# Sample attention in twenty steps of 512 keys in place of forty of 256, with a ring of fourteen key/value tiles

## The chip, the core and the metric

The kernel runs on one core of a Trainium2 chip. The metric is the device time of one execution in microseconds (us). The core has a matrix engine (PE, with its weight loads shown apart as PEld), a vector engine (DVE), a scalar engine (ACT), GpSimd (POOL), and SyncE (SP), which issues most direct DMA transfers. Indirect transfers (gathers) are issued by POOL. Each engine works through its own instructions in a fixed order and waits where an operand isn't there yet.

## The reference, cut to what matters

The kernel computes one inference step of a hybrid layer: a joint input projection, RWKV-7 heads, attention heads with three branches (compressed, selected, window), an output projection with layer norm, and a PEER expert mixer with layer norm. There are 256 prompt tokens and 8 sample sequences of 4 new tokens with 2048 past tokens each. All arithmetic here is fp32. The change touches the selected and the window branch of the sample's attention:

```python
s = jnp.einsum('bqkgd,bqknld->bqkgnl', q_c, k_g)             # selected blocks
kpos = top_idx[..., None] * SEL_BLOCK + jnp.arange(SEL_BLOCK)
m = (top_val >= 0)[..., None] & (kpos <= qpos[None, :, None, None, None])
p_s = masked_softmax(s.reshape(B, qc, NSA_KV_HEADS, NSA_GROUP, top_n * SEL_BLOCK), ...)
o_sel = jnp.einsum('bqkgnl,bqknld->bqkgd', p_s..., v_g)
...
s = jnp.einsum('bqkgd,bjkd->bqkgj', q_c, wkv[:, :, 0])         # window of 512
p_w = masked_softmax(s, m[None, :, None, None, :])
o_win = jnp.einsum('bqkgj,bjkd->bqkgd', p_w.astype(dt), wkv[:, :, 1])
return g_c[..., 0:1] * o_cmp + g_c[..., 1:2] * o_sel + g_c[..., 2:3] * o_win
```

The kernel scores all 2048 past keys of a sequence, and adds to each score a bias that is very negative for blocks that were not selected, so the selected branch is 2048 past keys (and 4 new ones) with a mask; the window branch is 512 past keys and the new ones.

## The kernel before, in words

**Stages.** The program is a row of stages. In each, several streams of work (Python generators) are interleaved by `weave` according to weights: that gives the program's order, which is a priority. A list scheduler with a model of each engine's time then sets the order on each engine, keeping dependences, the number of buffers of each pool, and the PSUM banks. So a change of a step can move instructions of another stream.

**The stage of the change** (marked W3, lines 1562 to 1580) weaves two streams: the sample's attention (`sample_late`: first steps, compressed branch, then `sample_attention`) with weight 137, and the RWKV states and steps of the sample (`sample_states`, `sample_steps`, lines 1205 to 1310) with weight 54. In the profiled execution it runs from about 561 to about 763 us. The next stage (W4) attends the prompt's tokens and begins the output projection.

**Tiles of the attention.** Sequences are taken in four pairs (`bp`), and a pair has 8 steps of 256 selected keys and 2 steps of 256 window keys: 40 steps. A tile `co` is 128 partitions by 1024: 256 positions of one sequence, two positions to a partition (e = 0, 1), with keys of 4 heads in columns 0 to 255 and values in 256 to 511 of each. A step has two such tiles, one for each sequence of the pair (b2). Selected tiles come by a gather on POOL (line 448), window tiles by a direct transfer on SP (line 894). They live in a ring of 10 tiles, 4 in one pool and 6 (`NCX`) in another; a step asks for the tiles of up to two steps ahead (`NAHEAD`) when its keys are turned.

**A step**, with its lines:

- `keys`: four transposes a sequence on PE (two head pairs kp, two positions e, line 918) into a PSUM bank `sa`, then one copy of 128x512 to `kt` (line 919): by DVE for the first sequence, by ACT for the second.
- `scored`: four matmuls (b2, kp), each 32 query rows in a column group of PE of its own, into one bank `sc` (line 937); in the last step of a branch four more against the new keys (line 940), into the same bank. DVE spreads the bias (line 931), adds it and takes the maximum (line 941, 945), negates it (line 947 or 949); ACT takes the exponential and its sum (line 951), into `S`.
- `applied`: PE turns the weights (two transposes, line 960) into bank `st`, ACT copies them to `pt` (line 962, 964), PE multiplies them with the values (eight matmuls, line 968) into bank `sao`, and ACT copies the result to `Oc` (line 970).
- At the end of a branch the parts are merged by their maxima on DVE (line 974 to 981, one call of line 981 for each step); at the end of a pair of sequences `heads` turns the result (line 990 to 997).

The order in the stream is keys(i+1), applied(i), scored(i+1). PSUM has banks ss=2 (for the states), sa=2, sc=1, st=1, sao=2. The states' and steps' lines on PE are 1217, 1232, 1259, 1288, 1297 and 1305, all into `ss`; POOL makes a masked product for line 1297 at line 1295.

**SP's row** in this stage: states in (`big`, line 1213, two batches), the prompt's x for the next stage (line 1627), window tiles, states out (line 1310), and the gate's weights `cw` for the next stage (lines 1413, 1414).

Of the kernel before, what the change touches and what calls it, by code (L numbers as in the profile page):

```python
# [14 lines left out]
AF = mybir.ActivationFunctionType  # L15
# [19 lines left out]
NAHEAD = 2  # L35
# [8 lines left out]
NCX = 6  # L44
# [23 lines left out]
def _const_table():  # L68
# [50 lines left out]
    for kk in range(4):  # L119
        wm[:, 0, kk % 2, kk // 2] = np.where(kk >= i + 1, 0.0, NEG)  # L120
# [26 lines left out]
def hybrid_decode_step(ctx: ExitStack, tc: tile.TileContext, a, outs, dbg=None):  # L147
# [299 lines left out]
    def gather(dst, rows_, ix):  # L447
        gp.indirect_dma_start(out=dst, out_offset=None, in_=rows_, in_offset=bass.IndirectOffsetOnAxis(ap=ix, axis=0))  # L448
# [431 lines left out]
    units = [(br, bp, ck) for bp in range(4) for br in "sw" for ck in range(2 if br == "w" else 8)]  # L880
# [3 lines left out]
    def load(i):  # L884

        br, bp, ck = units[i]
        tiles[i] = []
        for b2 in range(2):
            pool, n_ = rings[nload[0] % len(rings)]
            nload[0] += 1  # L890
            t_ = pool([P, 1024], "co", bufs=n_)
            if br == "w":
                src = a["state_win_kv"][0, 2 * bp + b2, 256 * ck:256 * ck + 256]
                sy.dma_start(t_, src.rearrange("(p e) a h d -> p (e a h d)", e=2))
            else:
                gather(t_, rows_s, sidx[:, 2 * bp + b2, ck:ck + 1])
            tiles[i].append(t_.rearrange("p (e c) -> p e c", e=2))

    def sample_attention(sp):


        kts, prob, outp = {}, {}, {}

        def kind(i):
            br, bp, ck = units[i]
            return br, bp, ck, (1, 2) if br == "w" else (0, 8)

        def keys(i):
            for i_ in range(i, min(i + 1 + NAHEAD, 40)):
                if i_ not in tiles:  # L910
                    load(i_)
            kts[i] = [sp([P, 2, 256], "kt", bufs=4) for b2 in range(2)]
            for b2 in range(2):
                pb = bank("sa")
                for kp in range(2):
                    for e in range(2):
                        o = 256 * kp + 128 * e
                        pe.transpose(pb[:, o:o + 128], tiles[i][b2][:, e, 128 * kp:128 * kp + 128], ident)  # L918
                (sc.copy if b2 else ve.tensor_copy)(kts[i][b2].rearrange("p k n -> p (k n)"), pb)

        def scored(i):
            br, bp, ck, (br_, nck) = kind(i)
            kt, new = kts.pop(i), ck == nck - 1
            if not ck:
                outp[br] = sp([P, 3, nck], "ST" + br), sp([P, nck, P], "Oc" + br)
            ST = outp[br][0]
            if br == "w":
                mk = C4("wmask")[:, 256 * ck:256 * ck + 256].rearrange("p (e k) -> p e k", e=2)
            else:
                BX = sp([P, 4, 32], "BX", bufs=2)  # L930
                ve.tensor_copy(BX, BI[:, bp, 4 * ck:4 * ck + 4, None].to_broadcast([P, 4, 32]))
                mk = BX.rearrange("p a b -> p (a b)")[:, None, :].to_broadcast([P, 2, P])
            mx2 = sp([P, 2], "mx2", bufs=3)
            S = prob[i] = sp([P, 288], "S", bufs=3)
            pb = bank("sc")
            for cg, (b2, kp) in enumerate(CG):
                pe.matmul(pb[32 * cg:32 * cg + 32, :256], q_of(2 * bp + b2, kp), kt[b2][:, kp, :], start=True, stop=True)
            if new:
                for cg, (b2, kp) in enumerate(CG):
                    pe.matmul(pb[32 * cg:32 * cg + 32, 256:288], q_of(2 * bp + b2, kp), KN[:, br_, kp, :], start=True, stop=True)  # L940
            ve.tensor_tensor_reduce(out=S[:, :256].rearrange("p (e k) -> p e k", e=2),
                                    in0=pb[:, :256].rearrange("p (e k) -> p e k", e=2),
                                    in1=mk, scale=1.0, scalar=NEG, op0=OP.add, op1=OP.max, accum_out=mx2[:, 0:1])
            if new:
                ve.tensor_tensor_reduce(out=S[:, 256:], in0=pb[:, 256:288], in1=C4("nmask")[:, 32 * bp:32 * bp + 32],
                                        scale=1.0, scalar=NEG, op0=OP.add, op1=OP.max, accum_out=mx2[:, 1:2])
                ve.tensor_scalar(ST[:, 0, ck:ck + 1], mx2[:, 0:1], mx2[:, 1:2], -1.0, op0=OP.max, op1=OP.mult)
            else:
                ve.tensor_scalar(ST[:, 0, ck:ck + 1], mx2[:, 0:1], -1.0, None, op0=OP.mult)
            n = 288 if new else 256  # L950
            sc.activation(S[:, :n], S[:, :n], AF.Exp, bias=ST[:, 0, ck:ck + 1], accum_out=ST[:, 1, ck:ck + 1])

        def applied(i):
            br, bp, ck, (br_, nck) = kind(i)
            S, tl, (ST, Oc), new = prob.pop(i), tiles[i], outp[br], ck == nck - 1
            tiles[i] = None
            po, pb = bank("sao"), bank("st")
            ks_ = [(0, P), (1, P)] + ([(2, 32)] if new else [])
            for k, w in ks_:
                pe.transpose(pb[:w, 128 * k:128 * k + 128], S[:, 128 * k:128 * k + w], ident)  # L960
            pt = sp([P, 384], "pt", bufs=2)
            sc.copy(pt[:, :256], pb[:, :256])
            if new:
                sc.copy(pt[:32, 256:], pb[:32, 256:384])
            for k, w in ks_:
                for cg, (b2, kp) in enumerate(CG):
                    rhs = tl[b2][:, k, 256 + 128 * kp:384 + 128 * kp] if k < 2 else VN[br_][:, 128 * kp:128 * kp + 128]
                    pe.matmul(po[32 * cg:32 * cg + 32, :P], pt[:w, 128 * k + 32 * cg:128 * k + 32 * cg + 32], rhs,
                              start=(k == 0), stop=(k == ks_[-1][0]))
            sc.copy(Oc[:, ck, :], po[:, :P])  # L970
            if new:
# [8 lines left out]
                for k in range(nck):  # L980
                    ve.scalar_tensor_tensor(Oa[:, bp, :], Oc[:, k, :], ST[:, 2, k:k + 1], Oa[:, bp, :],
                                            op0=OP.mult, op1=OP.add)
# [16 lines left out]
        for i in range(-1, 40):  # L999
# [6 lines left out]
            if i < 39:  # L1006
                scored(i + 1)
                yield 1
            if i % 10 == 2 and i < 30:
                yield from sample_compressed(sp, i // 10 + 1)  # L1010
            if i % 10 == 0 and i:
                heads(i // 10 - 1)
        heads(3)
# [551 lines left out]
    more_banks(sa=2, sc=1, st=1, sao=2)  # L1565
# [12 lines left out]
    weave((late, 137), (seq(sample_states(sx), sample_steps(sx)), 54))  # L1578
# [520 lines left out]
```

## Time and profile before

| | |
|---|---|
| median of 3 runs | 2595.13 us (2588.27 to 2599.22) |
| profiled execution | 2602.22 us, span 2600.4 us, mean PE clock 0.93 |
| PE busy | 2328.9 us, 90% of the span |
| PEld busy | 1961.5 us, 75% |
| DVE busy | 1955.5 us, 75% |
| ACT busy | 1027.7 us, 40% |
| POOL busy | 1281.1 us, 49% |
| the stage of the change, 561 to 763 us | PE 178.59, DVE 123.50, ACT 90.49, POOL 70.06 us busy of 202 |

The windows view tells by stretches how long each engine was busy; the groups view puts together instructions of one line, operation and shape; the timeline lists what follows what on each engine. A fp32 matmul appears as two records on PE, a transpose as one. A group's duration includes its drain, which can lie over the next group's start: what a group really holds of PE is read from start to start.

### The profile page before, as it was taken

The page shows a single profiled execution, that of the slowest core. Times are in us where ns is not written, and L with a number is a line of the kernel's source. Part 1 is how long each engine was busy: PE and PEld are TensorE (multiplying, and loading weights), DVE is VectorE, ACT ScalarE, POOL GpSimd, SP SyncE. Part 2 cuts the span into 40 slices and gives each one's busy share as a digit, 9 for nine tenths or more (in the row PEclk, how much of TensorE's full clock was granted, in tenths as well). Part 3 has the DMA queues.
Part 4 walks back from the last instruction along what each step waited for, and adds up shares of the span by engine and source line. Part 5 has one row for each costly group of instructions (what it writes and reads, how often), then busy time and mean ns, then how long its engine had stood idle before and what let it go on. Part 6 is the DMA issues. An engine that isn't in the chain of part 4 may idle for free.

```text
span 2600.4 us, 47649 instructions
## 1 busy us (share of the span) xinstructions
PE 2328.9 (90%) x17612; PEld 1961.5 (75%) x17612; DVE 1955.5 (75%) x4360; ACT 1027.7 (40%) x1932; POOL 1281.1 (49%) x1327
## 2 busy tenths in 40 slices
PE   7989999979989997469799999996699799989996
PEld 7877898865555655358699999995677688878885
DVE  4789756554742538949988888889976689878988
ACT  3433222224432332210244444443566544434443
POOL 5677423232510107635544444445555577767772
PEclk9989999988986997779899999997899999999998
DMA  7877964467656867886499999997778699899994
GB/s 222 241 218 241 275 199 139 130 200 223 213 178 234 275 243 245 312 267 172 153 371 349 352 352 346 352 338 225 232 241 294 233 324 326 319 336 322 325 322 174
DMA packets 346650, 683.49 MB, mean 263 GB/s; under 512 B 81338, under 2 KB 204785, under 8 KB 345361
## 3 DMA queue, kind: packets, MB, share of 16 engines
q1 hardware_dynamic: 251505, 344.67, 40.9%
q0 software_dynamic: 94912, 335.77, 36.9%
q8 instruction: 139, 2.28, 0.3%
q14 instruction: 94, 0.77, 0.1%
HBM read 664.77 MB, written 23.88 MB: 265 GB/s over the span
## 4 chain that ended last, share of the span: by engine, by line
PE 66%; DVE 17%; DMA 8%; issue 4%; POOL 3%; ACT 2%; SPq 0%; DVEq 0%; POOLq 0%; ACTq 0%
PE pb L2024 19%; PE ph L1832 14%; PE pj L417 6%; PE pt L1826 4%; DMA co<-in_cache_cmp_kv,gidx 2%; PE pj L1790 2%; PE pa L1650 2%; DVE rows L1756 2%; DVE CA L471 2%; PE ss L1478 2%; PE sa L918 1%; PE pa L1906 1%; PE p L1061 1%; PE px L1876 1%; PE fs L1924 1%
## 5 line engine op out<-in xcount | busy, mean ns | idle before, releaser
L448 POOL DMA_INDIRECT rq<-in_peer_v,gi x256 | 374.7, 1463 | 170.4 <-issue 80.7
L448 POOL DMA_INDIRECT rows<-in_peer_u,gi x256 | 298.6, 1166 | 313.3 <-DVE rows L1756 282.8
L1832 PE MATMUL ph<-XHd,ul 128*128 128x256 f32 x1024 | 304.6, 297 | 18.1 <-DVE ul L1622 18.1
L1756 DVE SCALAR_TENSOR_TENSOR rows<-rows,x1a 128x1024 f32<-128x1024 f32 x256 | 309.3, 1231 | 5.7 <-DMA rows<-in_peer_u,gi 5.5
L1832 PE MATMUL ph<-XHd,uh 128*128 128x256 f32 x1024 | 297.4, 290 | 0.3 <-ACT uh L1621 0.3
L1832 PE MATMUL ph<-XLd,uh 128*128 128x256 f32 x1024 | 290.7, 284 | 0.0
L1621 ACT CAST uh<-pt 128x512 fp32r<-128x512 f32 x256 | 149.8, 587 | 277.6 <-PE ph L1832 203.6
L417 PE MATMUL pj<-XH,wh 128*128 128x288 f32 (+1 forms) x752 | 230.4, 307 | 12.3 <-DVE ss L747 7.0
L417 PE MATMUL pj<-XH,wl 128*128 128x288 f32 (+1 forms) x752 | 232.2, 309 | 9.3 <-DVE wl L412 6.5
L1622 DVE TENSOR_TENSOR ul<-pt,uh 128x512 fp32r<-128x512 f32 x256 | 176.0, 689 | 80.8 <-ACT uh L1621 72.9
L417 PE MATMUL pj<-XL,wh 128*128 128x288 f32 (+1 forms) x752 | 226.7, 302 | 0.0
L2024 PE MATMUL pb<-vl,ah 128*128 128x512 f32 x768 | 217.7, 392 | 0.3 <-DVE vl L2018 0.3
L2024 PE MATMUL pb<-vh,al 128*128 128x512 f32 x768 | 216.4, 390 | 0.0
L2024 PE MATMUL pb<-vh,ah 128*128 128x512 f32 x768 | 199.1, 395 | 16.3 <-ACT vh L2017 16.3
L1832 PEld LDWEIGHTS ph<-XHd,ul 128*128 128x128 f32 x1024 | 196.7, 192 | 20.2 <-DVE ul L1622 20.0
L410 ACT CAST wh<-wraw 128x512 fp32r<-128x512 f32 (+1 forms) x188 | 114.8, 616 | 234.7 <-PE pj L417 180.2
L1832 PEld LDWEIGHTS ph<-XHd,uh 128*128 128x128 f32 x1024 | 197.3, 193 | 0.8 <-ACT uh L1621 0.5
L1832 PEld LDWEIGHTS ph<-XLd,uh 128*128 128x128 f32 x1024 | 197.0, 192 | 0.0
L1998 DVE SCALAR_TENSOR_TENSOR fP<-rq,ge,fP 128x512 f32<-128x512 f32 x254 | 189.9, 748 | 2.4
L2024 PEld LDWEIGHTS pb<-vh,ah 128*128 128x128 f32 x768 | 146.3, 191 | 47.7 <-ACT vh L2017 17.3
L471 DVE SCALAR_TENSOR_TENSOR CA<-co,wbc,CA 128x256 f32<-128x256 f32 x248 | 131.8, 570 | 55.8 <-DMA co<-in_cache_cmp_kv,gidx 55.6
L2024 PEld LDWEIGHTS pb<-vl,ah 128*128 128x128 f32 x768 | 145.8, 190 | 31.3 <-DVE vl L2018 0.7
(852 smaller groups left out, 5546.6 us busy)
## 6 DMA issues: line engine op xcount, KB each, us to landing
ur<-in_peer_u SPq DMA_DIRECT2D x128, 512.0 KB
wraw<-in_w_in SPq DMA_DIRECT2D x152, 256.0 KB
cw<-in_w_out SPq DMA_DIRECT2D x32, 512.0 KB
wraw<-in_w_out SPq DMA_DIRECT2D x32, 512.0 KB
cw<-in_peer_wq SPq DMA_DIRECT2D x32, 512.0 KB
wraw<-in_peer_wq SPq DMA_DIRECT2D x32, 512.0 KB
wraw<-in_w_in SPq DMA_DIRECT2D x64, 128.0 KB
co<-in_state_win_kv SPq DMA_DIRECT2D x16, 512.0 KB
```

Source lines behind the costliest of these rows:

```text
L410: sc.copy(wh[:, :, :n], w[:, :, :n])
L417: last[2] = pe.matmul(pb[:n, :nt], wi[:, k, :n], xi[(o + k) // 8][:, (o + k) % 8, :nt], start=(o + k == 0 and wi is wh and xi is xh), stop ...
L448: gp.indirect_dma_start(out=dst, out_offset=None, in_=rows_, in_offset=bass.IndirectOffsetOnAxis(ap=ix, axis=0))
L471: ve.scalar_tensor_tensor(d_, x_, w_, d_, op0=OP.mult, op1=OP.add)
L1478: pe.matmul(pb[32 * q:32 * q + 32, :256], lhs(k), w[:, 256 * q:256 * q + 256], start=(k % 4 == 0), stop=(k % 4 == 3))
L1621: sc.copy(xh, pb)
L1622: return ve.tensor_tensor(xl, pb, xh.bitcast(F32), OP.subtract)
L1756: i_ = ve.scalar_tensor_tensor(r_, r_, 1.0, X1a[t], op0=OP.mult, op1=OP.mult, accum_out=h_)
L1826: pe.transpose(pb[:, 128 * e:128 * e + 128], w[:, 512 * q + 128 * e:512 * q + 128 * e + 128], ident)
L1832: mm = pe.matmul(ph[:, :NPR], wi[:, e, :], xi[:, 4 * q + e, :NPR], start=(q == 0 and e == 0 and wi is wh and xi is XHd), stop=(q == 1 and ...
L1998: ve.scalar_tensor_tensor(fP[t], r_, w_, fP[t], op0=OP.mult, op1=OP.add)
L2024: pe.matmul(acc[3 * t + q], wi[:, P * t:P * t + P], xi[:, 512 * q:512 * q + 512], start=(k == 0 and wi is ah and xi is vh), stop=(k == P - ...
```

## The change

The steps become 512 keys: per pair of sequences four of the selected branch and one of the window, 20 in all, each with four tiles (i, b2, c), c being the half.

- `keys`: for each sequence and each head pair one bank `sa` with four transposes (e, c), and one copy of 128x512: DVE for the first head pair, ACT for the second.
- `scored`: the four matmuls are 32x512 and fill the bank `sc`; the new keys' four go to a bank `st`. One maximum over 512, one exponential over 512 (or 544), `S` has two buffers in place of three.
- `turned`: the turn of the weights is now a part of its own: four transposes, one copy of 128x512; the new keys' piece goes through a bank `sa`.
- `applied`: sixteen matmuls (or twenty) and one eviction; merges have half as many calls.
- The order in the stream is keys(i+1), turned(i−1), scored(i), applied(i−1), then the loads of four tiles. The ring has 14 tiles (`NCX` 10); fourteen are asked for at the start.
- The banks are ss=2, sa=3, sc=1, st=1, sao=1, and the weight of the stream is 78 in place of 137.

Line numbers of the changed kernel differ: before the function they are one lower, in the states and the later stages nine higher (1297 becomes 1306, 1213 becomes 1222, 1627 becomes 1636).

```diff
-NAHEAD = 2
...
-NCX = 6
+NCX = 10
...
-        wm[:, 0, kk % 2, kk // 2] = np.where(kk >= i + 1, 0.0, NEG)
+        wm[:, kk % 2, 0, kk // 2] = np.where(kk >= i + 1, 0.0, NEG)
...
-    units = [(br, bp, ck) for bp in range(4) for br in "sw" for ck in range(2 if br == "w" else 8)]
+    units = [(br, bp, u) for bp in range(4) for br in "sw" for u in range(1 if br == "w" else 4)]
+    pieces = [(i, b2, c) for i in range(len(units)) for c in range(2) for b2 in range(2)]
...
+    def loads(upto):
+
+        for i, b2, c in pieces[nload[0]:upto]:
...
-            kts[i] = [sp([P, 2, 256], "kt", bufs=4) for b2 in range(2)]
+            kts[i] = [sp([P, 2, 512], "kt", bufs=4) for b2 in range(2)]
             for b2 in range(2):
-                pb = bank("sa")
                 for kp in range(2):
-                    for e in range(2):
-                        o = 256 * kp + 128 * e
-                        pe.transpose(pb[:, o:o + 128], tiles[i][b2][:, e, 128 * kp:128 * kp + 128], ident)
-                (sc.copy if b2 else ve.tensor_copy)(kts[i][b2].rearrange("p k n -> p (k n)"), pb)
+                    pb = bank("sa")
+                    for n, (e, c) in enumerate(EC):
+                        pe.transpose(pb[:, 128 * n:128 * n + 128], tiles[i, b2, c][:, e, 128 * kp:128 * kp + 128], ident)
+                    (sc.copy if kp else ve.tensor_copy)(kts[i][b2][:, kp, :], pb)
...
-            S = prob[i] = sp([P, 288], "S", bufs=3)
+            S = prob[i] = sp([P, 544], "S", bufs=2)
             pb = bank("sc")
             for cg, (b2, kp) in enumerate(CG):
-                pe.matmul(pb[32 * cg:32 * cg + 32, :256], q_of(2 * bp + b2, kp), kt[b2][:, kp, :], start=True, stop=True)
+                pe.matmul(pb[32 * cg:32 * cg + 32, :], q_of(2 * bp + b2, kp), kt[b2][:, kp, :], start=True, stop=True)
             if new:
+                pn = bank("st")
...
+        def turned(i):
+            br, bp, u, (br_, nu) = kind(i)
+            S, pt = prob.pop(i), sp([P, 640], "pt", bufs=2)
+            pb = bank("st")
+            for k in range(4):
+                pe.transpose(pb[:, 128 * k:128 * k + 128], S[:, 128 * k:128 * k + 128], ident)
+            sc.copy(pt[:, :512], pb)
...
+        loads(len(rings))
+        for i in range(-1, 21):
+            if i < 19:
                 keys(i + 1)
                 yield 1
-            if i >= 0:
-                applied(i)
+            if i > 0:
+                turned(i - 1)
+            if 0 <= i < 20:
+                scored(i)
                 yield 1
-            if i < 39:
-                scored(i + 1)
+            if i > 0:
+                applied(i - 1)
+                loads(4 * i + len(rings))
                 yield 1
...
-    more_banks(sa=2, sc=1, st=1, sao=2)
+    more_banks(sa=3, sc=1, st=1, sao=1)
...
-    weave((late, 137), (seq(sample_states(sx), sample_steps(sx)), 54))
+    weave((late, 78), (seq(sample_states(sx), sample_steps(sx)), 54))
```

**Order on PE, in the last third of the stage.** A row is a run of instructions of one kind: line, operation, output and input names, shape, and how many. Before, around the state products of line 1297:

```order
L937 MATMUL sc<-kt,Qb 32x256 x2
L918 MATMUL sa<-CT_61,co 128x128 x4
L937 MATMUL sc<-kt,Qb 32x256 x2
L918 MATMUL sa<-CT_61,co 128x128 x8
L937 MATMUL sc<-kt,Qb 32x256 x4
L918 MATMUL sa<-CT_61,co 128x128 x4
L1297 MATMUL ss<-uvm,UB 64x512
```

and with the change, at the end of those products:

```order
L914 MATMUL sa<-CT_61,co 128x128 x7
L933 MATMUL sc<-kt,Qb 32x512
L914 MATMUL sa<-CT_61,co 128x128
L933 MATMUL sc<-kt,Qb 32x512
L914 MATMUL sa<-CT_61,co 128x128 x3
L1314 MATMUL ss<-CT_61,S0T 128x128 x3
L914 MATMUL sa<-CT_61,co 128x128 x4
L933 MATMUL sc<-kt,Qb 32x512
L914 MATMUL sa<-CT_61,co 128x128
L933 MATMUL sc<-kt,Qb 32x512
```

A step's four scores stood in one run or in two pairs; here each of the four stands by itself, between transposes of keys.

**Order on SP, over the whole stage.** Before (`x_00` to `x_11` are the prompt's x, `co` the window tiles):

```order
L1213 DMA big<-in_state_rwkv 64x4x64 x16
L1627 DMA x_00_10095<-in_x_prompt 128x1024
L1627 DMA x_01_10096<-in_x_prompt 128x1024
L1627 DMA x_10_10097<-in_x_prompt 128x1024
L1627 DMA x_11_10098<-in_x_prompt 128x1024
L1213 DMA big<-in_state_rwkv 64x4x64 x16
L894 DMA co<-in_state_win_kv 128x1024 x12
```

and with the change, its start and its end apart:

```order
L1222 DMA big<-in_state_rwkv 64x4x64 x32
L893 DMA co<-in_state_win_kv 128x1024 x12
```

```order
L1319 DMA out<-S_9538 64x4x64 x4
L1636 DMA x_00_9719<-in_x_prompt 128x1024
L1636 DMA x_01_9720<-in_x_prompt 128x1024
L1636 DMA x_10_9721<-in_x_prompt 128x1024
L1636 DMA x_11_9722<-in_x_prompt 128x1024
L1422 DMA cw<-in_rwkv_g 128x1024
L1423 DMA cw<-in_rwkv_g 32x1024
```

The four x transfers moved from between the two batches of states to behind the last states out, just ahead of the gate's weights.

More of the change, by code (lines that the diff above doesn't have):

```diff
@@ L879, in hybrid_decode_step @@
     tiles, ends = {}, {}
[L880 removed]
+    units = [(br, bp, u) for bp in range(4) for br in "sw" for u in range(1 if br == "w" else 4)]
+    pieces = [(i, b2, c) for i in range(len(units)) for c in range(2) for b2 in range(2)]
     rings, nload = [(na, NCO)] * NCO, [0]
[L884 to L888, printed above, removed]
+    def loads(upto):
+        for i, b2, c in pieces[nload[0]:upto]:
+            br, bp, u = units[i]
             pool, n_ = rings[nload[0] % len(rings)]
@@ L899, in sample_attention @@
+            tiles[i, b2, c] = t_.rearrange("p (e c) -> p e c", e=2)
     def sample_attention(sp):
-        kts, prob, outp = {}, {}, {}
+        kts, prob, outp, turned_ = {}, {}, {}, {}
+        EC = [(e, c) for e in range(2) for c in range(2)]
         def kind(i):
-            br, bp, ck = units[i]
-            return br, bp, ck, (1, 2) if br == "w" else (0, 8)
+            br, bp, u = units[i]
+            return br, bp, u, (1, 1) if br == "w" else (0, 4)
         def keys(i):
-            for i_ in range(i, min(i + 1 + NAHEAD, 40)):
-                if i_ not in tiles:
-                    load(i_)
-            kts[i] = [sp([P, 2, 256], "kt", bufs=4) for b2 in range(2)]
+            kts[i] = [sp([P, 2, 512], "kt", bufs=4) for b2 in range(2)]
@@ L953, in applied @@
-        def applied(i):
[L954 to L965, printed above, removed]
-                for cg, (b2, kp) in enumerate(CG):
-                    rhs = tl[b2][:, k, 256 + 128 * kp:384 + 128 * kp] if k < 2 else VN[br_][:, 128 * kp:128 * kp + 128]
+                ve.tensor_scalar(ST[:, 0, u:u + 1], mx2[:, 0:1], -1.0, None, op0=OP.mult)
@@ new lines, in scored @@
+            n = 544 if new else 512
+            sc.activation(S[:, :n], S[:, :n], AF.Exp, bias=ST[:, 0, u:u + 1], accum_out=ST[:, 1, u:u + 1])
+        def turned(i):
+            br, bp, u, (br_, nu) = kind(i)
+            S, pt = prob.pop(i), sp([P, 640], "pt", bufs=2)
[3 more added lines that the diff above has]
+            sc.copy(pt[:, :512], pb)
+            if u == nu - 1:
+                pn = bank("sa")
+                pe.transpose(pn[:32, :128], S[:, 512:], ident)
+                sc.copy(pt[:32, 512:], pn[:32, :128])
+            turned_[i] = pt
@@ new lines, in applied @@
+        def applied(i):
+            br, bp, u, (br_, nu) = kind(i)
+            pt, (ST, Oc), new = turned_.pop(i), outp[br], u == nu - 1
+            po = bank("sao")
+            for k in range(5 if new else 4):
+                for cg, (b2, kp) in enumerate(CG):
+                    if k < 4:
+                        e, c = EC[k]
+                        w, rhs = P, tiles[i, b2, c][:, e, 256 + 128 * kp:384 + 128 * kp]
+                    else:
+                        w, rhs = 32, VN[br_][:, 128 * kp:128 * kp + 128]
@@ L968, in applied @@
                     pe.matmul(po[32 * cg:32 * cg + 32, :P], pt[:w, 128 * k + 32 * cg:128 * k + 32 * cg + 32], rhs,
-                              start=(k == 0), stop=(k == ks_[-1][0]))
-            sc.copy(Oc[:, ck, :], po[:, :P])
+                              start=(k == 0), stop=(k == (4 if new else 3)))
+            sc.copy(Oc[:, u, :], po[:, :P])
             if new:
```

46 lines of the change are left out of this document (19 added, 27 removed).

## The prediction, made before the result was known

> **What bounds the kernel now.** The change lies in one stage, the sample's attention woven with the RWKV steps of the sample (about 561 to 763 us of the profiled execution), so I read that stage first, in the table of windows. Its columns are the stretch, its length, the busy us (and instruction count) of PE, PEld, DVE, ACT and POOL, then PE's granted clock, the DMA share and GB/s.
>
> ```profile
> core 0: us, PE busy (x) PEld busy (x) DVE busy (x) ACT busy (x) POOL busy (x), PEclk, DMA share, GB/s
> ...
> 581.00:591.00 10.00, 5.43 (x58) 3.51 (x57) 2.99 (x17) 3.32 (x13) 4.05 (x5) 0.74 1.01 265
> ...
> 631.00:641.00 10.00, 10.00 (x162) 6.74 (x162) 4.22 (x24) 4.67 (x18) 3.75 (x4) 1.00 0.58 187
> ...
> 721.00:731.00 10.00, 7.92 (x85) 4.89 (x89) 3.63 (x16) 4.77 (x14) 5.19 (x6) 1.00 1.02 346
> 731.00:741.00 10.00, 8.54 (x95) 4.58 (x89) 3.58 (x13) 5.56 (x16) 2.29 (x3) 1.00 1.02 357
> ...
> 751.00:763.00 12.00, 6.26 (x94) 3.94 (x83) 11.46 (x50) 4.17 (x14) 0.00 (x0) 0.87 0.41 98
> sum 202.00, PE 178.59 PEld 104.00 DVE 123.50 ACT 90.49 POOL 70.06; mean PE 8.93 PEld 5.20 DVE 6.18 ACT 4.52 POOL 3.50
> ```
>
> PE is busy 178.59 of 202 us; DVE (123.5) and ACT (90.5) are far from full. The 23.4 us in which PE stands still are gathered in a few places: where the DMA share is 1.0 (581 to 591, 721 to 741) and in the tail, where DVE alone works (11.46 of 12 us). Next the groups of instructions of that stage, to see what PE and its helpers do for the attention (after the bar: busy us, mean ns | idle just before, and what ended it):
>
> ```profile
> L918 PE MATMUL sa<-CT,co 128*128 128x128 f32 x320 | 54.6, 299 | 4.9 <-issue 2.9 <-DVE kt L919 1.6 <-DMA co<-in_cache_sel_kv,sidx 0.2
> L448 POOL DMA_INDIRECT co<-in_cache_sel_kv,sidx x56 | 53.5, 955 | 86.5 <-PE sao L968 70.1 <-issue 6.3 <-PE st L960 4.2
> L937 PE MATMUL sc<-kt,Qb 128*32 128x256 f32 x320 | 43.0, 404 | 2.1 <-DVE mx L941 0.7 <-issue 0.4 <-ACT kt L919 0.4
> L968 PE MATMUL sao<-co,pt 128*32 128x128 f32 x640 | 28.8, 285 | 2.8 <-ACT pt L962 2.7
> L960 PE MATMUL st<-CT,S 128*128 128x128 f32 (+1 forms) x88 | 17.8, 291 | 6.0 <-ACT S L951 4.5 <-DVE STs L949 1.5
> ...
> L951 ACT ACTIVATE S<-S,STs 128x256 f32<-128x256 f32 (+1 forms) x32 | 16.4, 512 | 14.0 <-DVE STs L949 11.2 <-issue 1.1 <-DVE s L538 0.9
> L962 ACT COPY pt<-st 128x256 f32<-128x256 f32 x40 | 15.0, 375 | 11.9 <-PE st L960 8.6 <-PE sc L937 1.5 <-ACT S L951 0.6
> L941 DVE CUSTOM_DVE_ANT_1 S<-sc,BX 128x256 f32<-128x256 f32 x32 | 13.4, 420 | 29.0 <-PE sc L937 16.4 <-PE sa L918 5.6 <-PE sc L940 3.9
> L981 DVE SCALAR_TENSOR_TENSOR Oa<-Ocs,STs,Oa 128x128 f32<-128x128 f32 x32 | 12.1, 379 | 1.8 <-ACT Ocs L970 1.2
> ```
>
> PE's waits for this chain are small: 6.0 us before the turn (L960), 2.8 before the apply (L968), 2.1 before the scores (L937). The stage is bound by how much PE does, with some idle for data. So the sum is made in PE time, and the last view is PE's timeline, whose starts show what a group really occupies (the second column includes the drain, which overlaps the next group):
>
> ```profile
> 704.14 1.09 PE L918 MATMUL sa<-CT,co 128*128 128x128 f32 x8
> ...
> 705.17 1.07 PE L1297 MATMUL ss<-uvm,UB 64*64 64x512 f32 x2
> ...
> 706.16 0.64 PE L968 MATMUL sao<-co,pt 128*32 128x128 f32 x16
> ...
> 709.86 0.64 PE L937 MATMUL sc<-kt,Qb 128*32 128x256 f32 x8
> ...
> 710.42 0.66 PE L918 MATMUL sa<-CT,co 128*128 128x128 f32 x4
> ```
>
> ```profile
> 727.19 0.63 PE L937 MATMUL sc<-kt,Qb 128*32 128x256 f32 x4 [0.22 <-DVE kt L919]
> ...
> 727.75 0.66 PE L918 MATMUL sa<-CT,co 128*128 128x128 f32 x4
> ...
> 728.34 0.64 PE L968 MATMUL sao<-co,pt 128*32 128x128 f32 x16
> ...
> 728.91 0.44 PE L960 MATMUL st<-CT,S 128*128 128x128 f32 x2
> ...
> 729.18 0.60 PE L1305 MATMUL ss<-CT,S0T 128*128 128x128 f32 x4
> ```
>
> An fp32 matmul leaves two records, a transpose one. Four scores side by side (x8) hold PE from 709.86 to 710.42, 0.56 us; two (x4) from 727.19 to 727.75, also 0.56. **A group of scores costs the same however many of the four column groups are in it**, and the transposes behind it start only when it is over.
>
> **The change part by part.** *Scores.* Before, one copy hands over both head pairs of a batch, so a step's four scores come out of the order in one group (16 steps) or in two pairs (24 steps): 16 + 48 = 64 groups, times 0.56 = 35.8 us. Now each copy hands over one head pair of one batch, with four transposes between, and a score is 512 wide. Counted in the order of the changed kernel, 7 steps fall into four singles, 6 into a pair and two singles, 3 into two pairs, 4 stay whole: 28 + 18 + 6 + 4 = 56 groups. A two-pass 512-wide matmul holds PE from 705.17 to 706.16, 0.99 us (L1297, the nearest row; a 256-wide score at 0.56 doubled would be 1.12). 56 × 0.99 = 55.4. Against 35.8 that is **+19.6 us**. Had all twenty stayed whole it would be 20 × 0.99 = 19.8, a gain of 16. This is the term that decides: half as many steps, but nearly as many groups, each twice as long.
>
> [...]
>
> *Keys.* 320 transposes as before. Eight hold PE 1.03 us (704.14 to 705.17), four 0.59 (727.75 to 728.34), so four more cost 0.44, and a group has some 0.15 of its own. The order has 87 groups in place of 74: 13 × 0.15 = **+2.0**. *Turn and apply.* Turning goes from 40 groups to 30 of the same transposes, −10 × 0.15 = **−1.5** (two hold PE 0.27, 728.91 to 729.18: below the fit, so it may be less). Applying goes from 41 groups to 33, at the same 0.15 **−1.2**; a bound on the other side is that eight groups' full 0.57 (728.34 to 728.91) minus their work were saved, some −3. *New keys* now go to a bank of their own and stand alone eight times: 8 × 0.15 = **+1.2** at most. Sum on PE: 19.6 + 2.0 − 1.5 − 1.2 + 0.6 (half of the new keys' bound) = +19.5; with the favourable ends of turn and apply, and a few neighbouring scores overlapping their drain, +15. I take **+17**: 178.6 becomes some 196 us.
>
> *DVE and ACT.* Maximum, exponential, eviction and merge run 20 times in place of 40. Per step the fixed part goes: a merge (L981) does half its 32 calls less, 6 us; the maximum, exponential and turned eviction double in width and save only their overhead. Altogether perhaps 17 us on each of DVE and ACT. All of it lies under PE (123.5 and 90.5 of 202 busy); only where PE waits for this chain does it show, 6.0 + 2.8 + 2.1 us at most by the groups above. The new place of the turn (behind the next keys, one step later) aims at the same 10.9 us. Against it stands a longer tail: the last step's turn, apply, merge and head transposes follow each other over 512 keys, in a stretch where DVE was already the bound (11.46 of 12). I book −6 for the waits and +4 for tail and start (first scores need four tiles of keys in place of two): **−2**.
>
> *Ring.* Fourteen tiles, requested four at a time after an apply. The gathers are the same 56 and the window loads the same 16, so bytes don't change, and the two stretches at DMA share 1.02 stay as they are.
>
> ```profile
> 732.31 0.94 POOL L448 DMA_INDIRECT co<-in_cache_sel_kv,sidx  x1 [0.88 <-PE sao L968]
> ...
> 733.55 0.93 POOL L448 DMA_INDIRECT co<-in_cache_sel_kv,sidx  x1 [0.30 <-PE st L960]
> ```
>
> POOL issues a gather each 1.24 us (732.31 to 733.55), so four take 5 us, and PE has some 10 us a step (202/20). What is queued behind them on POOL is the masked product for the state steps (L1295), which waits up to 5 us for a burst; PE's state matmuls (L1297) have the attention to cover that. I book **0**, and price the other case below.
>
> *Queue of SP.* The prompt's x loads, 2 MB (L1627), move from the stage's start to its end:
>
> ```profile
> 565.82 4.94 SPq L1627 DMA_DIRECT2D x<-in_x_prompt  x4
> ...
> 757.14 0.48 SPq L1413 DMA_DIRECT2D cw<-in_rwkv_g  x1
> 761.59 0.34 SPq L1414 DMA_DIRECT2D cw<-in_rwkv_g  x1
> ```
>
> At the start they shared the DMA engines with the first tiles, which is a gain of a few us there; now they hold SP 4.94 us ahead of the weights of the next stage's gate (cw), which bounds the loss at 5. I book **0**, ±3.
>
> Total: 17 − 2 = **+15 us** on the profiled execution's 2602.2 us (its span is 2600.4), that is 2617. That execution was 7 us above the median 2595.1 of the runs shown, so I state **2610** on the median's basis.
>
> **The rivals.** *Faster: a lone score runs beside its neighbours.* If a score on one column group overlapped the transposes or state matmuls around it, what counts would be passes of the widest column group: 20 × 0.99 = 19.8 against 35.8, −16, and with −2 for waits and −2 for turn and apply some −20: **2575**. It decides when a score group's mean start-to-start time falls under 0.49: 56 × 0.49 = 27.4, 8.4 under the 35.8 of before, and the other terms (−2.6 on PE, −2 in waits) make it 13. For it: column groups do overlap among themselves. Against: behind a pair the transposes started only after the whole 0.56.
>
> *No difference: the added PE time falls into idle.* PE stands still 23.4 us. If DVE's and ACT's lighter load and the later turn close all the 10.9 us of waits and half of the DMA-bound idle, 17 − 11 − 5 leaves about 0 to +3: **2597**. For it: the list order put other work into most gaps already. Against: the idle lies at DMA share 1.0 and in the tail, where neither helps.
>
> *Much slower: the ring stalls.* Fourteen tiles hold three and a half steps; half of a step's tiles are asked for only after an apply that now comes a step later.
>
> ```profile
> POOL co L448 <- PE sao L968: 70.1, 14, 16.7
> ...
> 994.91 6.23 DMA cw<-in_peer_u,gi
> ```
>
> POOL waited 70.1 us for applies already (harmlessly), and a gather of another stage took 6.23 us to land when it stood on the path. If the last two tiles of each of some 16 steps come 2 us late, that is +30 on top: **2640**. Against: in the order, an apply and the first use of the tile it frees are mostly seven or more us of PE work apart, by the group prices above.
>
> **How the numbers follow.** Likeliest (PE pays for single scores): 0.47, 2610, own range 2600 to 2628. Overlap: 0.19, 2575. Absorbed: 0.22, 2597. Ring: 0.12, 2640. About 0.5%, 13 us, is what a measurement here tells from no change; 2582 to 2608 is "within". Slower is the ring and three quarters of the likeliest, 0.12 + 0.35 = 0.47; faster the overlap, with a little of it left inside, 0.18; the rest, 0.35, is within. The range reaches from 2584 (most of the absorbed case, not the overlap) to 2635 (not the full ring case).
>
> **What would show it.** Right: in the stage's windows PE busy near 195 with DVE near 106 and ACT near 73; the scores' line in the timeline mostly as x2 groups of 128x512, each about 1 us from the next start; the stage some 15 us longer; everything behind it shifted by that. Wrong: a single score's next instruction starting 0.3 us later (overlap); PE idle under 10 us with PE busy near 195 (absorbed); long "DMA co" releasers before key transposes (ring); a change in the stages behind 763 us larger than that in this one.

## The result, and the profile after

The changed kernel took 2628.4 us (median of 4 runs, 2622.4 to 2634.0), the kernel before on the same chip 2595.4 us. The ratio is 1.0127 (95% interval 1.0102 to 1.0152): slower by 33 us, where +15 was forecast. The two profiled executions differ by less, 2625.8 against 2600.4 us of span, 25.4 us. The table shows where these lie, by the first rows of PE's lines in both traces:

| piece | before, us | after, us | difference |
|---|---|---|---|
| up to the stage | 559.9 | 558.8 | −1.1 |
| the stage of the change (to the first instruction of the next stage) | 202.1 | 214.1 | +12.0 |
| from there to the sample's first gate product (L1454, after L1463) | 2.8 | 11.7 | +8.9 |
| from the gate product to the end of the sample's layer norm (first L1352, after L1361) | 205.1 | 205.3 | +0.1 |
| from there to the end of the last PE product | 1608.2 | 1613.5 | +5.3 |

So the loss has two places: the stage itself, and the 12 us behind it. First the stage. The windows view over the whole of it, before and after (columns as in the prediction; the last three are PE's granted clock, DMA share and GB/s):

```profile
560.00:762.00 202.00, 178.79 (x1971) 104.71 (x1972) 123.87 (x499) 90.11 (x273) 70.81 (x74) 0.93 0.71 226
```

```profile
558.00:773.00 215.00, 197.62 (x1816) 104.71 (x1816) 107.22 (x387) 77.36 (x193) 71.52 (x73) 0.94 0.59 198
```

PE is busy 197.6 us in place of 178.8, DVE and ACT lost 16.7 and 12.8, PE's idle went from 23.2 to 17.4. The groups of the changed kernel, to be set beside those of before:

```profile
L933 PE MATMUL sc<-kt,Qb 128*32 128x512 f32 x160 | 61.0, 617 | 0.0
L914 PE MATMUL sa<-CT,co 128*128 128x128 f32 x320 | 56.9, 296 | 3.5 <-DVE kt L915 1.7 <-issue 0.8 <-DMA co<-in_cache_sel_kv,sidx 0.7
...
L974 PE MATMUL sao<-co,pt 128*32 128x128 f32 x640 | 25.5, 283 | 2.6 <-ACT pt L956 1.4 <-DVE Oa L571 0.7 <-ACT Ocs L976 0.5
...
L955 PE MATMUL st<-CT,S 128*128 128x128 f32 x80 | 13.3, 286 | 2.8 <-ACT S L948 1.6 <-DVE YNs L1003 1.0
```

Half as many records of scores (160 for 320) take 61.0 us in place of 43.0; keys take 2.3 more, apply 3.3 less, turn 4.5 less (without the eight small pieces of the new keys, which now have a line of their own). The wait ahead of the turn fell from 6.0 to 2.8 us, and keys waited 0.7 us for tiles: the ring is no bound. What a single score costs, PE's timeline near the end of the stage shows:

```profile
755.45 1.04 PE L933 MATMUL sc<-kt,Qb 128*32 128x512 f32 x2
756.42 0.33 PE L914 MATMUL sa<-CT,co 128*128 128x128 f32 x1
756.68 1.05 PE L933 MATMUL sc<-kt,Qb 128*32 128x512 f32 x2
757.66 1.20 PE L914 MATMUL sa<-CT,co 128*128 128x128 f32 x9
...
759.90 1.05 PE L933 MATMUL sc<-kt,Qb 128*32 128x512 f32 x4
760.89 0.98 PE L914 MATMUL sa<-CT,co 128*128 128x128 f32 x7
```

One score (x2) holds PE from 755.45 to 756.42, 0.97 us; two side by side (x4) from 759.90 to 760.89, 0.99. The price of a group was right.

Behind the stage, SP's queue and what held it:

```profile
751.00 14.63 SPq L1319 DMA_DIRECT2D out<-S  x11
773.12 2.43 SPq L1636 DMA_DIRECT2D x<-in_x_prompt  x4
775.64 0.47 SPq L1422 DMA_DIRECT2D cw<-in_rwkv_g  x1
776.21 0.39 SPq L1423 DMA_DIRECT2D cw<-in_rwkv_g  x1
```

```profile
SPq L1636 <- PE st L998: 7.4, 1, 7.4
```

SP was done with the states at 765.6, and then stood 7.4 us at the first load of x, waiting for PE's L998, the very last head transpose of the stage; cw queued behind it until 775.64. (In the program's memory map the first x tile now begins 64 bytes a partition inside the tile `od` that L998 reads; before, it met only tiles that were long free.) On PE meanwhile:

```profile
775.21 3.58 PE L642 MATMUL sa<-cb,QT 64*128 64x8 f32 x16
...
779.07 3.58 PE L642 MATMUL sa<-cb,QT 64*128 64x8 f32 x16
...
784.58 0.64 PE L1463 MATMUL ss<-sg,cw 128*128 128x32 f32 x2 [1.93 <-DMA cw<-in_rwkv_g]
```

and before:

```profile
764.70 0.48 PE L1454 MATMUL ss<-sg,cw 128*128 128x32 f32 x2
...
773.90 2.31 PE L643 MATMUL sa<-cb,QT 64*128 64x8 f32 x20
```

Before, the gate products came first and the prompt's 32 compressed scores (L643) after them; now the scores stand in front (L642, twice 3.6 us), and then the gate product still waits 1.93 us for cw. The sample's chain (gate, output projection, layer norm, expert queries) begins with that product. The last product of the expert queries (L1799, before L1790) starts 23 us later than before (1273.5 for 1250.3 us), whereas the prompt's layer norm behind its output projection (L1718, before L1709) starts 1.2 us earlier: the delay comes by the sample's chain.

### The profile page after: what moved, and what is told of

Read it like the earlier page. It is cut to its first block, busy times and chain, and to the rows that moved or that the text cites. A ratio compares the mean times of both kernels' runs of the same rounds, so it can differ in the third digit from the quotient of the medians.

```text
span 2625.8 us, 47111 instructions
## 1 busy us (share of the span) xinstructions
PE 2344.8 (89%) x17452; PEld 1962.0 (75%) x17452; DVE 1940.8 (74%) x4264; ACT 1014.7 (39%) x1852; POOL 1284.7 (49%) x1327
## 4 chain that ended last, share of the span: by engine, by line
PE 67%; DVE 13%; DMA 8%; issue 5%; POOL 4%; ACT 2%; SPq 1%; DVEq 0%; POOLq 0%; ACTq 0%
PE pb L2033 19%; PE ph L1841 13%; PE pj L416 6%; PE pt L1835 4%; DMA co<-in_cache_cmp_kv,gidx 3%; PE pa L1659 2%; PE sc L933 2%; PE sa L914 2%; DVE rows L1765 2%; PE p L1070 1%; PE pa L1915 1%; PE pj L1799 1%; DVE CA L470 1%; PE px L1885 1%; PE ss L1487 1%
```

## The experiments

Two theories were tried: that the stage is bound by PE and a group of scores costs about a microsecond whatever is in it (the prediction's), and that the rest of the loss is the sample's chain that starts late. Rivals: the stage is bound by idle, ring or chain; the next stage is longer for another reason. Medians are compared with those of the kernel before, run beside each version on the same chip; between chips that kernel ranged from 2585.6 to 2598.9 us. So versions that ran beside each other (`gap` with `whole` and `whole_gap`; `after_again`, the changed kernel unaltered, with `gap_gate_again` and `cw_first_again`) can be set against each other, and the rest only by their ratios, loosely.

**gap.** Only x's place in memory.

```diff
+    lp([P, 32], "gap")
     X1 = [[lp([P, 1024], f"x1_{t}{h}") for h in range(2)] for t in range(2)]
```

> The change, with 128 bytes a partition left free ahead of the prompt's x tiles, so that they no longer share 64 bytes with the tile of the last head transposes; every engine's order stays the same. Theory (half of the loss arises behind the stage: x waits on SP for the last head transposes, and the gate's weights cw wait behind it): the stage ends as in the changed kernel, about 773 us, but SP issues x near 766 in place of 773.1, the first gate product (L1463) starts near 776 in place of 784.6, and the whole is 6 to 9 us shorter, about 2620. Rival (the next stage is longer because its list order changed): L1463 may come earlier, the total stays at 2628 within 2.

Measured: 2631.9 us, ratio 1.0128 (1.0093 to 1.0163), against the 2620 expected. No gain is seen, though an interval of 9 us either way would not exclude a small one. SP and PE of this kernel:

```profile
771.96 1.97 SPq L1637 DMA_DIRECT2D x<-in_x_prompt  x4
774.04 0.59 SPq L1422 DMA_DIRECT2D cw<-in_rwkv_g  x1
```

```profile
782.66 3.58 PE L642 MATMUL sa<-cb,QT 64*128 64x8 f32 x16
...
786.51 3.58 PE L642 MATMUL sa<-cb,QT 64*128 64x8 f32 x16
790.02 0.63 PE L1463 MATMUL ss<-sg,cw 128*128 128x32 f32 x2
```

x no longer waits (its end at 773.9 is 6 us before the stage's, 779.8), and the gate product no longer waits for cw; but it starts 10.2 us behind the stage all the same, because the order on PE puts L642 first. The theory that the wait on SP alone was the cause falls: it was one of two locks, and the other stayed.

**whole.** The four scores of a step as one row on PE, by scheduling alone: the score on the copy that comes last goes first, and each of the others is queued behind the one before it (`behind`, an order without a wait).

```diff
-            for cg, (b2, kp) in enumerate(CG):
-                pe.matmul(pb[32 * cg:32 * cg + 32, :], q_of(2 * bp + b2, kp), kt[b2][:, kp, :], start=True, stop=True)
+            m_ = None
+            for cg, (b2, kp) in sorted(enumerate(CG), key=lambda c_: (-c_[1][0], -c_[1][1])):
+                with tc.high_priority(offset=2000):
+                    n_ = pe.matmul(pb[32 * cg:32 * cg + 32, :], q_of(2 * bp + b2, kp), kt[b2][:, kp, :], start=True, stop=True)
+                m_ = behind(n_, m_)
```

> The change, with the four scores of a step put in one row on PE (scheduling order only, high priority, no extra wait on data). In its order the scores are 22 groups in place of 56 and the keys 68 in place of 87. Theory (PE is the bound and a group of scores costs 0.98 us however many column groups it has): scores hold PE about 22 us in place of 55, the stage is 25 to 35 us shorter, the total about 2598 (2590 to 2606). Rival (the stage is held by tiles that come late, or by the chain through maximum and exponential): PE's busy time in the stage falls by as much, but idle takes its place, and the total stays above 2618.

Measured: 2610.8 us, ratio 1.0048 (1.0027 to 1.0069), 21 us under `gap` beside it, whose stage has the changed kernel's order. The time lies between the theory's 2598 and the rival's 2618. Groups and window:

```profile
L941 PE MATMUL sc<-kt,Qb 128*32 128x512 f32 x160 | 24.8, 648 | 3.1 <-issue 2.6 <-ACT kt L921 0.5
```

```profile
561.00:762.00 201.00, 171.41 (x1810) 109.19 (x1809) 109.96 (x387) 76.55 (x193) 70.44 (x73) 0.88 0.63 211
```

The scores fell from 61.0 to 24.8 us and the stage from 214 to 201, 13 us where 25 to 35 were expected. The score groups, with the fewer key groups that the same order brings (68 for 87), account for the stage's loss. But PE busy fell by 26 us, not by 36, and the granted clock from 0.94 to 0.88; this comes back below.

**whole_gap**, both edits.

> Both edits together: scores of a step in one row, and the free bytes ahead of the x tiles. If the two losses are independent, as the theory says, their gains add: about 2590 (2582 to 2598), just under the kernel before. If one hides the other (the next stage is bound by something else as soon as cw comes early), the gain is that of the scores alone, about 2598.

Measured: 2608.7 us, 1.0045 (1.0020 to 1.0070): as `whole`, and some 11 us over the higher of the two times expected. This is consistent with `gap`, which has no gain to add.

**gap_gate** and **gap_gate_again**: `gap`, and L642 behind the gate products.

```diff
+            gate.append(pe.matmul(o, g2b[64:96, js], sg1[64:96, NPR:], start=False, stop=True))
...
+                        with tc.issue_after(gate[-1].ins):
                             pe.matmul(bk[par][:, 32 * kp + 8 * g:32 * kp + 8 * g + 8], QT[hs[par], kp, g, tok],
```

> The kernel 'gap' (x tiles moved by 128 bytes), and on PE the prompt's 32 compressed scores of the next stage (L642) put behind the sample's gate products (L1463, L1464), as they stood before the change. In 'gap' alone nothing was won: cw came early, but PE had L642 to do first, 2 x 3.6 us. Theory (two locks on the first gate product, and the sample's chain behind it sets the end): L1463 starts 3 to 4 us after the end of the stage in place of 10 to 12, the sample's last product of w_out (L1487) moves by as much, the total is 6 to 9 us under 'gap', about 2622. Rival (the sample's chain has slack): L1463 comes early, the total stays.

> The changed kernel again, unaltered, so that the next three stand beside it on one chip: some 30 to 33 us over the kernel before.

> x tiles moved by 128 bytes and the gate products ahead of L642 on PE, beside the changed kernel on the same chip. Theory (the late gate products cost what the stage does not explain): 7 to 11 us under the changed kernel. Rival (the gap seen between two chips is the chips'): within 3 of it.

Measured: 2609.9 us, 1.0102 (1.0065 to 1.0138), on another chip than `gap`; so it ran again beside the changed kernel. There the changed kernel (`after_again`) took 2621.7 (1.0147, 1.0119 to 1.0174), `gap_gate_again` 2610.0 (1.0112, 1.0082 to 1.0143): 11.7 us less by the medians, 9 by the ratios, whose intervals overlap. PE of the second run:

```profile
763.88 0.46 PE L1679 MATMUL pa<-CT,SHO 128*108 128x128 f32 x1
764.70 0.41 PE L1679 MATMUL pa<-CT,SHO 128*27 128x128 f32 x1 [0.35 <-ACT wraw L1680]
764.90 0.47 PE L1466 MATMUL ss<-sg,cw 128*128 128x32 f32 x2
```

The gate product (L1466 here) starts 3.5 us behind the end of the stage (761.4) in place of 10.5 in `after_again`.

**cw_first** and **cw_first_again**: the loads of x written behind those of cw; the scheduler then puts the gate products ahead of L642 by itself.

```diff
-    for t in range(2):
-        for h in range(2):
-            with tc.issue_after(ends[2].ins):
-                sy.dma_start(X1[t][h], ...)
...
         gate_rows(g2a, g2b)
+        prompt_x()
```

> The change, with the loads of x written behind the loads of cw, so that cw is ahead of x on SP; the scheduler then also puts the gate products ahead of L642, as in the kernel before. Theory: as 'gap_gate', L1463 some 3 us behind the end of the stage, total about 2620, 8 us under the changed kernel. Rival: 2628 within 3.

> cw ahead of x on SP, beside the changed kernel on the same chip. Theory: 7 to 11 us under the changed kernel, as the other way to the same order. Rival: within 3 of it.

Measured: 2607.3 (1.0074, 1.0050 to 1.0099) and 2614.8 (1.0108, 1.0078 to 1.0138), the second 6.9 us under the changed kernel beside it. The gate product starts 2.8 us behind the stage in both. So in the changed kernel both edits that start the sample's chain early give back 7 to 12 us by the medians, and the one that leaves it late shows no gain. The profiles bear this out in part: from the end of the stage to the sample's layer norm, the three with a late gate product (the changed kernel twice, `gap`) took 216 to 217 us, `gap_gate`, `gap_gate_again` and `cw_first` 209 to 212, but `cw_first_again` 220. In that last one the whole early start was lost again on the way, and the profile does not show where its gain in the median arose.

**before_late**: the reverse, in the kernel before: gate products queued behind L643.

```diff
+            if not qt:
+                tc.add_manual_dep(gate[0].ins, m_.ins.name, ...)
```

> The kernel before, with the one thing put in that the changed kernel has behind the stage: the gate products queued on PE behind the 32 compressed scores of the prompt. Theory (this order alone costs what the stage does not explain): the stage stays at 202 us, the first gate product (L1454) starts 8 to 9 us later, and the total is 6 to 10 us longer, about 2604. Rival (the sample's chain has slack): total within 3 of before.

Measured: 2604.2 us against 2585.6, ratio 1.0062 (1.0038 to 1.0086): slower by 16 to 19 us, more than the 6 to 10 expected. PE:

```profile
752.05 3.58 PE L643 MATMUL sa<-cb,QT 64*128 64x8 f32 x16
755.56 0.41 PE L1670 MATMUL pa<-CT,SHO 128*27 128x128 f32 x1
755.90 3.58 PE L643 MATMUL sa<-cb,QT 64*128 64x8 f32 x16
759.42 0.63 PE L1458 MATMUL ss<-sg,cw 128*128 128x32 f32 x2
```

The product starts 10.2 us behind the stage, 7.5 later than before; in the stage that follows, the chain to the layer norm took 218 us in place of 205, with 1305 PE records from the end of the stage to that layer norm in place of 1213. One moved run of products reshuffled the stage behind it, so this run does not price the late start alone.

**whole_cw** and **whole_gate**: both causes taken away at once.

> Scores of a step in one row, and cw ahead of x on SP (gate products ahead of L642 on PE). Theory: the gains of 'whole' (stage 201 us) and 'cw_first' add: about 2602, the chain of the sample starting 3 us behind the stage. Rival (in 'whole' the 8 us late start was given back before 970 us): 2609, as 'whole'.

> The change with scores in one row, x tiles moved by 128 bytes and the gate products ahead of L642. Theory (these two causes are the loss): stage about 201 us with about 50 us at half rate, the first gate product 3 to 4 us behind it, the total within 8 us of the kernel before. Rival (a third cause behind the stage): 15 or more over it.

Measured: `whole_cw` 2619.5 (1.0107, 1.0072 to 1.0142), worse than `whole`, against the theory; `whole_gate` 2610.0 against 2598.9 (1.0033, 1.0012 to 1.0054), 3 to 14 us over the kernel before, between the 8 of the theory and the 15 of the rival. The stage of `whole_gate` took 207 us, 60 of them at half rate, where 201 and 50 were expected. In `whole_cw` the gate product came 2.2 us behind the stage, as meant, but the chain to the layer norm took 224 us where `whole` took 197, with almost the same number of PE records from the stage to it (1305 and 1306). One thing that differs is the clock: from the end of the stage to 1000 us PE was at half rate for 96 us in `whole_cw` and for 55 in `whole` (how half-rate time is worked out stands below). That this is the cause is not shown; each version has one profile.

**before_whole** and **before_whole_again**: scores in one row in the kernel before (the same edit, 256 wide), 40 groups for 64.

> The kernel before, with the four scores of a step in one row: 40 groups in place of 64. Theory: 24 groups by 0.54 us less on PE, 13 us; the stage 8 to 13 us shorter, the total about 2585. Rival (idle in the stage takes the place): 2595 within 3.

> The kernel before with the scores of a step in one row, once more, to narrow the interval of its gain: by the stage's 8 us in its first profile, 4 to 10 us under the kernel before.

Measured: 2595.4 against 2597.4 (0.9975, 0.9942 to 1.0007), then 2603.9 against 2587.5 (1.0075, 1.0047 to 1.0103). The first is no clear gain where about 2585 us was expected, the second a loss of 16 where 4 to 10 were to be won; the two intervals do not meet, though it is one program. So an interval here holds for its own chip and hour, and a difference of under 1% between versions that did not run beside each other shows nothing. In one profile the stage gained 8 us, in the other it lost 9:

```profile
559.00:753.00 194.00, 167.19 (x1974) 103.39 (x1973) 123.16 (x499) 88.88 (x273) 71.75 (x74) 0.91 0.75 236
```

```profile
551.00:763.00 212.00, 182.92 (x1974) 113.86 (x1973) 125.43 (x499) 89.81 (x273) 71.88 (x75) 0.83 0.69 217
```

Work and counts are the same; PE's clock is 0.91 and 0.83. No version is faster than the kernel before beyond its interval.

**before_plain** and **before_double**: the kernel before for a second profile, and with each step's scores computed twice (the second group of four overwrites the first).

```diff
+            for _ in range(2):
                 for cg, (b2, kp) in enumerate(CG):
```

> The kernel before, unaltered, for a second profile: within 3 us of itself; the stage between 197 and 202 us, its half-rate time 23 to 28 us.

> The kernel before, in which each step's four scores are computed twice, the second time as one more group of four. Theory (PE bounds the stage, a group of scores costs 0.53 to 0.56 us whatever it holds): 40 more groups, PE busy +21 us in the stage, the stage 18 to 21 us longer; no more half-rate time than before. Rival (the stage is bound by idle, clock or the chain, PE has room): stage longer by less than 8 us.

Measured: `before_plain` 2598.9 (0.9994, 0.9973 to 1.0016), but its profile, at 2612.4 of span, has a stage of 221 us:

```profile
557.00:779.00 222.00, 197.87 (x1974) 115.75 (x1973) 124.28 (x499) 90.84 (x273) 71.38 (x75) 0.83 0.65 206
```

`before_double` 2630.7 against 2598.9 (1.0111, 1.0081 to 1.0140):

```profile
L938 PE MATMUL sc<-kt,Qb 128*32 128x256 f32 x640 | 64.1, 407 | 4.8 <-ACT kt L919 2.0 <-issue 1.0 <-DVE mx L942 0.8
```

```profile
560.00:781.00 221.00, 205.13 (x2291) 120.30 (x2291) 123.91 (x499) 89.86 (x273) 70.68 (x74) 0.89 0.66 207
```

Forty more groups of scores raise the scores' line from 43.0 to 64.1 us, 0.53 each by the records, and PE's busy time to 205. By the starts it is less, since an added group mostly stands right behind the first:

```profile
658.49 1.07 PE L938 MATMUL sc<-kt,Qb 128*32 128x256 f32 x16
659.49 0.66 PE L918 MATMUL sa<-CT,co 128*128 128x128 f32 x4
```

Eight scores hold PE 1.00 us where four hold 0.57, so an added group costs 0.43 and forty some 17 us. The stage is 19 us longer than the 202 of the first profile of before, and about as long as that of `before_plain`, whose clock was lower. Of the 32 us of the total, what lies behind the stage is not the scores': the chain from the gate product to the layer norm took 226 us in place of 205, with 1305 PE records from the stage to its end in place of 1213, so here too the order of the next stage had changed.

To compare the stages, the half-rate time has to be taken out. The granted clock is either full or half in the traces (those of before and after have 32 stretches at 1.0 and 32 at 0.5 each), so the time at half rate is twice (1 − clock) times the length. That is 28 us in the first profile of before and 75 in `before_plain`; the stage grew by 20 us over these 47, so 0.42 us for each us at half rate. The two profiles of `before_whole` give 0.49 (18 us over 37). Brought to 25 us at half rate by 0.42, an estimate, the stages are: before 201, changed 214 (26 us at half rate), `whole` 191 (48), `before_whole` 190 (35) and 192 (72), `before_double` 211 (49). The other profiles show how far to trust this: the seven whose stage has the changed kernel's order come to 209 to 215, the three with the order of before to 198 to 201, the four of the changed kernel with scores in one row to 186 to 192. So at one clock the score groups cost, to within some 5 us: 40 groups in `before_double` +10 for 17 us of PE; the change +13 for 19 us; putting them in one row −23 (`whole`) for 36 and −9 to −11 (`before_whole`) for 13. Roughly half to four fifths of the PE time shows in the stage, the rest lies in what was idle.

## Why the prediction was right or wrong

**Scores, the term that decides: right.** 56 groups by 0.99 was forecast as 55.4 us; the groups in the order were those, their price 0.97 to 0.99, and the line grew by 18.0 (43.0 to 61.0). PE went from 178.8 to 197.6, +18.8, where +17 was taken and +19.5 worked out. The rival that a lone score runs beside the transposes or state products around it is refuted (0.97 for one, next start behind it).

One part of the price of a group the prediction did not tell apart, though it does not move the sum: what stands behind the group. In the first profile of before, four scores hold PE 0.57 us when transposes follow them and 0.45 when products of their own 128x32 shape do (medians of 8 and 4 such places at full clock: 0.57 and 0.46):

```profile
649.41 0.64 PE L937 MATMUL sc<-kt,Qb 128*32 128x256 f32 x8
649.98 0.66 PE L918 MATMUL sa<-CT,co 128*128 128x128 f32 x4
```

```profile
651.95 0.64 PE L937 MATMUL sc<-kt,Qb 128*32 128x256 f32 x8
652.40 0.62 PE L968 MATMUL sao<-co,pt 128*32 128x128 f32 x16
```

Four transposes likewise hold it 0.49 when more transposes follow and 0.59 when a 128x32 product does (medians of 12 and 23 places). So some 0.1 us of such a group's 0.57 came with another shape behind it. The price was read between transposes and held it already. In the changed kernel a lone score held PE 0.98 us in all 37 places at full clock where a product of another shape follows. In the two places where 128x32 applies stand around it (615.39 and 665.59 us) two scores and the apply between them took 0.96 us together. Two smaller slips: the limit of 0.49 for a measurable gain takes −2.6 on PE for the other terms where the sum has −0.1 (with that it would be some 0.45), and in the tail where DVE "alone" works, PE is busy 6.26 of 12 us by the row shown. Nothing hangs on either.

**DVE, ACT and waits: right in kind, off in size.** DVE and ACT lost 16.7 and 12.8 us and it was worth little: the stage grew by 12.0 of 18.8, so 6 to 7 us came back, of which the wait ahead of the turn is 3.2. I had booked −2 in the sum: the size was off by 4 to 5, to the good. The rival by which the idle absorbs all is refuted: PE's idle went from 23.2 to 17.4 us, not under 10.

**Ring: right.** Keys waited 0.7 us for gathered tiles; the ring rival did not come.

**The step that failed: "Queue of SP … I book 0, ±3"**, with 5 as the bound of the loss. Measured, the first gate product came 8.9 us later in relation to the stage, and edits that undo it gave 7 to 12 us by the medians. The prediction's own sign of being wrong, "a change in the stages behind 763 us larger than that in this one", came true: 14.3 us behind the stage against 12.0 in it. Two things were mis-sized. The bound counted the 4.94 us of SP that the four loads hold, but not a wait of the first of them for memory: the tile had moved under one that is read last, and cw stood behind it 7.4 us. And the order of the next stage was open to reading: L642 stood ahead of L1463 in the changed kernel and not before, 2 × 3.6 us on PE, ahead of the sample's chain. Of the two the order is the larger: behind L642, PE waited for cw only 1.93 us more, and 0.19 in `after_again`. `cw_first` shows what brought the order about: with cw ahead of x on SP, the scheduler puts the gate products first again. I had read SP's row and the stage's rows, and not carried the question "who waits for that" through the next stage to its end.

**What remains.** Stage +12 and gate +9 make 21 of the 25.4 between the two profiles; another 5 lie behind 970 us, among differences of half-rate time (102 against 82 us between 1000 and 1260), and are not explained (in `after_again` that piece took 1610.0 us, 2 over before). The remaining distance from 25 to the 33 of the medians is that the one profiled execution of before was 7 us over its median, which I had carried along as if both kernels would sit alike above it; that of after was at its median. `whole_gate`, without either cause, is still 3 to 14 us over before. Whether that is the longer half-rate time of its stage (60 us against 28), the order of the next stage (1269 PE records from the stage to the layer norm against 1213) or a third cause is not settled. Nor is it settled why the early gate product, worth 7 to 12 us in the changed kernel, shows no gain once the scores stand in one row (`whole` against `whole_cw` and `whole_gate`): these did not run beside each other, and the half-rate time behind the stage differed by up to 41 us between their profiles. How much the late gate product costs is therefore known less well than that it came late.

The stated range held by luck: it was drawn wide to reach towards the ring case, which did not come. The sum for the likeliest, +15 for a measured 33, was short by half, for the reasons above.

## What to carry to other kernels

Count groups, not instructions: here one score of 512 keys held PE 0.97 us and two side by side 0.99, so an edit that halves the steps but has each operand handed over by its own copy can cost more than it saves (64 groups of 0.56 us became 56 of 0.98). Read the order of the changed program until the chain that sets the end is met again: the first product of the next stage was part of the change. And where a pool grows, look at which tile of the next stage now lies under it: 64 shared bytes held SP's queue for 7.4 us, and undoing that wait alone showed no gain, as a second lock stood behind it.

## What the runs showed of the hardware that was not expected

The same program has stages of 202 and 222 us, with PE's granted clock at 0.93 and 0.83. The windows around two falls to half rate, first in the first profile of before, then in `before_plain`:

```profile
582.40:585.80 3.40, 1.30 (x21) 0.91 (x21) 0.07 (x1) 1.13 (x5) 2.66 (x3) 1.00 1.11 293
585.80:592.60 6.80, 5.71 (x42) 3.46 (x44) 2.40 (x15) 1.12 (x3) 0.94 (x1) 0.50 1.06 288
```

```profile
603.50:606.90 3.40, 3.08 (x66) 2.76 (x63) 1.60 (x11) 1.47 (x5) 1.10 (x2) 0.99 0.61 172
606.90:658.10 51.20, 51.20 (x450) 32.09 (x448) 17.27 (x76) 13.65 (x44) 9.39 (x10) 0.50 0.33 108
```

The first fall follows 3.4 us in which PE was busy 1.30. The second follows 3.4 us in which PE was busy 3.08, some 1.8 of them with 64x8 products of the states (L1232), and then the clock stood at 0.50 for 51.2 us although PE's records fill every one of them. So little work ahead of the fall is not what the two share, and work back to back did not end the half rate within 51.2 us. The two stretches, 6.8 and 51.2 us, are 2 and 15 times 3.41 us. In the traces of before and after the stretches at 0.50, but for the last, which ends with the trace, are whole multiples of it too: 31 in each, from 3.41 to 64.85 us. What makes the clock fall and what brings it back, no run here shows.

This may be part of why taking work from PE gave less than the work: the four profiles of the changed kernel with scores in one row have 49 to 61 us at half rate in the stage, the seven with the changed kernel's own order 11 to 29. But the kernel before went from 28 to 75 us by itself, so that less work on PE brings more time at half rate is not shown.
